# A log-sum-exp over rows: which row comes in two parts, and where its parts arrive

## The chip, the cores and the metric

The kernel runs on one core of a Trainium2 chip. The metric is the device time of one execution in microseconds (us), the median of several runs. The core has a matrix engine (PE), a vector engine (DVE), a scalar engine for exponentials and logarithms (ACT), a general engine (POOL) and a queue engine (SP) that issues the transfers (DMA) between the chip's memory and the on-chip buffer SBUF. SBUF has 128 partitions; a small second buffer, PSUM, takes PE's results and some of ACT's.

## The reference

The input is 32 x 512 rows of 1024 numbers in fp32, 64 MiB. The output is one number for each of the 16384 rows, the logarithm of the sum of the exponentials:

```python
max_x = np.max(x, axis=-1, keepdims=True)
return (max_x.squeeze(-1) + np.log(np.sum(np.exp(x - max_x), axis=-1))).astype(np.float32)
```

The kernel computes log(sum(exp(x))) without taking the maximum off, and checks beside it that the sums lie in a range where this is exact enough. Where the check fails, a second path behind a branch computes all rows again with the maximum. With this input it isn't taken.

## The kernel before

**Tiling.** Each of the 128 partitions holds 128 rows, called columns here (NC = 128), so 512 KB. Before the change the rows lie in memory as two pieces: the first 128 x 112 rows, of which each partition takes 112 in a row (W = 112; neighbouring partitions start 448 KB apart), and the last 128 x 16, of which each takes 16 (B = 16; 64 KB apart). Lines 78 to 86 make the two views of the input and of the output.

**Loads.** LOADS (lines 23 to 27) lists 18 loads with a size in columns and a string of operations. The sizes shrink towards the end, from 16 columns to 0.46875. A load may end within a row; the rest of the row then comes with the next load. All loads are issued by SP in this order (line 139), into a ring of 48 columns in SBUF. A load into a part of the ring first waits for the engine that used it last (`users`, lines 135 to 137). All loads go through one queue and their data come in the order of issue.

**Operations.** For each load ACT waits until it has landed and takes the exponential in place, one instruction for each operation of the string (line 228). The last operation of a load takes all that has landed, its partial row too. Then the rows are summed:

- `R7`: DVE sums 7 rows with one reduction (line 239).
- `F6`: POOL adds the second halves of 6 rows to the first (line 233), and DVE sums the halves later (`reduce_folded`, line 171).
- `T3`: for each of 3 rows DVE adds both halves and accumulates the sum in one instruction (line 249); PE adds the sums of the last rows into `count` for the check.
- `Y`, `Z`: the last row (column 127) comes in two loads. ACT takes the exponential of each part into PSUM and accumulates its sum, `first_sum` or `last_sum` (line 202). DVE copies `first_sum` to `sumexp` (line 212).

**Logarithms and stores.** Once column LATE = 119 is reached, ACT takes the logarithm of the first 112 columns (line 268), DVE runs the early half of the check (lines 146, 151), and SP stores these results (line 276). After the last load ACT takes the logarithm of 15 more columns (line 279), and then of the last row, where the sum of its first part comes in as the bias (line 281):

```python
ln_last = act.did(nc.scalar.activation(
    out=res[:, LAST:NC], in_=last_sum, func=AF.Ln, bias=sumexp[:, LAST:NC]
))
```

SP stores the last 16 columns (line 285), 64 bytes a partition and 8 KB in a row in memory. DVE and PE run the rest of the check (lines 290 to 308); ACT and DVE read its result, and SP waits for both (line 365), for the early store (366) and for the last one (369).

**Order.** Each engine runs its instructions in the order of the program and waits on semaphores; `Counted` counts what an engine has done, and `wait` makes another engine wait for a count.

Of the kernel before, what the change touches and what calls it, by code (L numbers as in the profile page):

```python
# [16 lines left out]
B = 16  # L17
LATE = 119
# [3 lines left out]

LOADS = [
# [29 lines left out]
def kernel(  # L53
# [5 lines left out]
    nc = tc.nc  # L59
# [24 lines left out]
    def source(e0, size):  # L84
        assert e0 >= W * d or e0 + size <= W * d
        return x_rest[:, e0 - W * d : e0 - W * d + size] if e0 >= W * d else x_rows[:, e0 : e0 + size]

    loads = [
        (int(size * d), [(op[0], 0 if op[0] == "Y" else int(op[1:] or 1)) for op in ops.split()])
        for size, ops in LOADS  # L90
    ]
    assert sum(size for size, _ in loads) == NC * d
    assert sum(s for _, ops in loads for _, s in ops) == NC
# [9 lines left out]
    over = sbuf("over", d)  # L103
# [5 lines left out]
    last_exp = nc.alloc_psum_tensor("last_exp", [P, d], fp32).ap()  # L109
# [24 lines left out]
    def load(i, here, done_before, size):  # L134
        for a, b, who, at in users:
            if a < here + size and b > here:
                sp.wait(who, at)
        users[:] = [u for u in users if not (u[0] < here + size and u[1] > here)]
        return nc.sync.dma_start(
            out=ring[:, here : here + size], in_=source(done_before, size)  # L140
        ).then_inc(landed[i], 16)

    def check_early():
        dve.wait(act, summed_by_act)
        dve.wait(dve, dve.n)
        dve.did(nc.vector.tensor_scalar(  # L146
            out=clamped[:, 0:LATE], in0=sumexp[:, 0:LATE],
            scalar1=LOW, scalar2=HIGH, op0=ALU.max, op1=ALU.min,
        ))
        dve.wait(dve, dve.n)  # L150
        dve.did(nc.vector.scalar_tensor_tensor(  # L151
            out=clamped[:, 0:LATE], in0=clamped[:, 0:LATE], scalar=0.0, in1=sumexp[:, 0:LATE],
            op0=ALU.bypass, op1=ALU.not_equal, accum_out=bad[:, 0:1],
        ))
        pe.wait(dve, dve.n)
        pe.did(nc.tensor.matmul(count, lhsT=bad[:, 0:1], rhs=far, start=True, stop=False))  # L156

# [6 lines left out]
    def reduce_folded():  # L164

        nonlocal early_sum
        while folded:
            c0, s0, p0, n0 = folded.pop(0)
            halves = ring[:, p0 : p0 + s0 * d].rearrange("p (c d) -> p c d", d=d)[:, :, 0:H]
            dve.wait(pool, n0)  # L170
            at = dve.did(nc.vector.reduce_sum(  # L171
                out=sumexp[:, c0 : c0 + s0], in_=halves, axis=AX.X
            ))
            users.append((p0, p0 + s0 * d, dve, at))
            if c0 < W:
                early_sum = at

    c = 0
    p = 0
    here = 0  # L180
    early_sum = 0
    done_before = 0
    summed_by_act = 0
    ln_early = None
    first_load = None
    for i, (size, ops) in enumerate(loads):
# [5 lines left out]
        dma = load(i, here, done_before, size)  # L192
        first_load = first_load or dma.ins
        end = here + size
        done_before += size
        act.wait(landed[i], 16)
        for k, (how, s) in enumerate(ops):
            rows = ring[:, p : p + s * d].rearrange("p (c d) -> p c d", d=d)
            if how in "YZ":

                assert c == LAST and (how == "Z" or here == p)
                at = act.did(nc.scalar.activation(  # L202
                    out=last_exp[:, here - p : end - p], in_=ring[:, here:end], func=AF.Exp,
                    accum_out=first_sum if how == "Y" else last_sum,
                ))
                if how == "Z":
                    last_piece = ring[:, here:end]
                here = end
                if how == "Y":
                    nc.vector.addr_align(128, offset=0, max_nops=0)  # L210
                    dve.wait(act, at)
                    first_piece = dve.did(nc.vector.tensor_copy(out=sumexp[:, LAST:NC], in_=first_sum))  # L212
                summed_by_act = at
            elif how == "A":
                assert here == p
                v = ring[:, p : p + d]
                at = act.did(nc.scalar.activation(
                    out=v, in_=v, func=AF.Exp, accum_out=sumexp[:, c : c + 1]
                ))
                here += d  # L220
                users.append((p, p + d, act, at))
                summed_by_act = at
                who = (act, at)
            else:
# [3 lines left out]
                at = act.did(nc.scalar.activation(out=v, in_=v, func=AF.Exp))  # L228
                here = upto
# [7 lines left out]
            elif how == "R":  # L237
                dve.wait(act, at)
                who = (dve, dve.did(nc.vector.reduce_sum(  # L239
                    out=sumexp[:, c : c + s], in_=rows, axis=AX.X  # L240
                )))
                users.append((p, p + s * d, *who))
            elif how == "T":
                if c >= W:
                    reduce_folded()
                dve.wait(act, at)
                for r in range(s):
                    lo = rows[:, r, 0:H]
                    who = (dve, dve.did(nc.vector.scalar_tensor_tensor(  # L249
                        out=lo, in0=lo, scalar=1.0, in1=rows[:, r, H:d],  # L250
                        op0=ALU.mult, op1=ALU.add, accum_out=sumexp[:, c + r : c + r + 1],
                    )))
                    users.append((p + r * d, p + (r + 1) * d, *who))
                    if c + r >= LATE:
                        add_up(c + r, who, start=False, stop=False)
            if how == "A" and c >= LATE:
                add_up(c, who, start=False, stop=False)
            if how in "RT":
                if c < W:
                    early_sum = dve.n  # L260
                reduce_folded()
            c += s
            p += s * d
            if c == LATE:

                act.wait(dve, early_sum)
                act.wait(act, early_act)
                ln_early = act.did(nc.scalar.activation(  # L268
                    out=res[:, 0:W], in_=sumexp[:, 0:W], func=AF.Ln
                ))  # L270
                check_early()
            if c <= W:
                early_act = summed_by_act
        assert here == end
    sp.wait(act, ln_early)
    nc.sync.dma_start(out=out_rows, in_=res[:, 0:W]).then_inc(sp.sem, 16)

    act.wait(dve, dve.n)
    act.did(nc.scalar.activation(out=res[:, W:LAST], in_=sumexp[:, W:LAST], func=AF.Ln))  # L279
    act.wait(act, summed_by_act)  # L280
    ln_last = act.did(nc.scalar.activation(  # L281
        out=res[:, LAST:NC], in_=last_sum, func=AF.Ln, bias=sumexp[:, LAST:NC]
    ))
    sp.wait(act, ln_last)
    nc.sync.dma_start(out=out_rest, in_=res[:, W:NC]).then_inc(stored, 16)
# [8 lines left out]
    add_up(LAST, (dve, first_piece), start=False, stop=False)  # L294
# [4 lines left out]
    half = last_piece.shape[1] // 2  # L299
# [19 lines left out]
    with nc.If(all_fine < 1):  # L319
# [5 lines left out]
        for c0 in range(0, NC, RING):  # L325
# [5 lines left out]
            edge = max(c0, min(W, c0 + s))  # L331
            for c1, c2 in ((c0, edge), (edge, c0 + s)):
                if c1 == c2:
                    continue
                nc.scalar.dma_start(
                    out=ring[:, (c1 - c0) * d : (c2 - c0) * d],
                    in_=source(c1 * d, (c2 - c1) * d),
                ).then_inc(again, 16)
                rows += 16
# [20 lines left out]
        nc.scalar.dma_start(out=out_rest, in_=res[:, W:NC]).then_inc(again, 16)  # L360
        nc.scalar.dma_start(out=out_rows, in_=res[:, 0:W]).then_inc(again, 16)
        nc.scalar.wait_ge(again, rows + 32)
# [60 lines left out]
```

## Time and profile before

| | us |
|---|---|
| median of 3 runs | 161.78 (161.76 to 161.81) |
| the profiled execution | 161.75 |
| its span, first to last instruction | 160.4 |
| ACT busy | 114.5 (71%) |
| DVE busy | 114.3 (71%) |
| POOL busy | 37.3 (23%) |
| PE busy | 2.2 (1%) |
| DMA, mean over the span | 419 GB/s |

The span is shorter than the device time by what lies around the instructions. In a list of groups, each line names the line of the kernel, the engine, the operation, what it writes and reads with the shapes, how often, the busy time, the mean of one in ns, and the idle time ahead of it with what ended it. In the chain of waits, the work that ended last is followed back from the end: each piece has its start, its duration and what ran. In the list of loads each line has the size and the time from the issue to the landing. In the waits of a queue, each line names who waited for whom: us in total, times, longest.

### The profile page before, as it was taken

To read this page: it belongs to the slowest core of one execution; us is meant where nothing else is said; L and a number is where in the kernel's file an instruction comes from. 1 tells how busy PE (TensorE), PEld (TensorE's weight loads), DVE (VectorE), ACT (ScalarE), POOL (GpSimd) and SP (SyncE) were. 2 spreads that over 40 slices of the span, in tenths; PEclk is the share of its full clock that TensorE was granted. 3 is DMA by queue.
4 is the path that set the end of the run, shared out by engine and by line. 5 is a ranking of instruction groups with operands and counts; after the bars stand their busy time and mean duration, and the time that the engine had idled before them with its cause. 6 is when DMAs were issued, how large, how long until landed. Compare 5 with 4: busy or idle time off the path is not lost.

```text
span 160.4 us, 219 instructions
## 1 busy us (share of the span) xinstructions
PE 2.2 (1%) x26; PEld 1.1 (1%) x26; DVE 114.3 (71%) x59; ACT 114.5 (71%) x31; POOL 37.3 (23%) x11
## 2 busy tenths in 40 slices
PE   0000000000000000000000000000000000000022
PEld 0000000000000000000000000000000000000011
DVE  0000000009999499994999859959999999999996
ACT  3000059990699708995099949991999989799996
POOL 0000000000000000000000994690004969891000
DMA  7996996996996996996999999999999999999992
GB/s 262 523 523 262 523 523 262 523 507 278 523 490 294 523 490 294 523 490 294 482 441 441 441 425 409 409 409 480 432 395 417 450 416 398 448 411 424 412 413 95
DMA packets 2881, 67.18 MB, mean 419 GB/s; under 512 B 576, under 2 KB 704, under 8 KB 1344
## 3 DMA queue, kind: packets, MB, share of 16 engines
q1 hardware_dynamic: 2880, 67.18, 97.7%
q14 instruction: 1, 0.01, 0.0%
HBM read 67.11 MB, written 0.07 MB: 419 GB/s over the span
## 4 chain that ended last, share of the span: by engine, by line
DMA 52%; ACT 28%; DVE 19%; issue 1%; PE 0%
DMA ring<-in_x_dram 52%; ACT ring L228 27%; DVE sumexp L239 15%; DVE sumexp L171 2%; DVE ring L249 1%; DVE over L301 0%; PE count L306 0%; ACT res L268 0%; DVE clamped L290 0%; DVE fine L308 0%; DVE sumexp L212 0%
## 5 line engine op out<-in xcount | busy, mean ns | idle before, releaser
L228 ACT ACTIVATE ring<-ring 128x16384 f32<-128x16384 f32 (+16 forms) x23 | 111.7, 4908 | 43.0 <-DMA ring<-in_x_dram 43.0
L239 DVE TENSOR_REDUCE sumexp<-ring 128x16 f32<-128x16384 f32 (+4 forms) x9 | 85.6, 9513 | 42.7 <-ACT ring L228 42.7
L233 POOL TENSOR_TENSOR ring<-ring 128x3072 f32<-128x3072 f32 (+3 forms) x7 | 37.1, 5313 | 107.3 <-ACT ring L228 107.3
L171 DVE TENSOR_REDUCE sumexp<-ring 128x6 f32<-128x3072 f32 (+3 forms) x7 | 18.4, 2656 | 0.0
L249 DVE SCALAR_TENSOR_TENSOR ring<-ring 128x512 f32<-128x512 f32 x15 | 9.6, 687 | 0.4 <-ACT ring L228 0.4
L125 ACT ACT_TABLE_LOAD x1 | 1.3, 1283 | 1.4 <-PEq L62 1.4
L156 PE MATMUL count<-far,bad 128*1 128x1 f32 x2 | 0.2, 164 | 153.2 <-DVE clamped L151 153.2
L160 PE MATMUL count<-sumexp,ones 128*1 128x1 f32 x18 | 1.6, 164 | 3.6 <-DVE ring L249 3.6
L249 DVE DVE_READ_ACCUMULATOR ring<-ring 128x1 f32 x15 | 1.2, 82 | 0.0
L202 ACT ACTIVATE last_exp<-ring 128x544 f32<-128x544 f32 (+1 forms) x2 | 1.2, 584 | 0.0
L126 DVE MEMSET ones<- 128x1 f32 x1 | 0.1, 59 | 1.5 <-PEq L62 1.5
L156 PEld LDWEIGHTS count<-far,bad 128*1 128x1 f32 x2 | 0.1, 80 | 153.2 <-DVE clamped L151 153.2
L160 PEld LDWEIGHTS count<-sumexp,ones 128*1 128x1 f32 x18 | 0.8, 80 | 4.5 <-DVE ring L249 4.5
L301 DVE SCALAR_TENSOR_TENSOR over<-ring 128x240 f32<-128x240 f32 x1 | 0.4, 404 | 0.0
L308 DVE TENSOR_SCALAR fine<-count 1x1 int32<-1x1 f32 x1 | 0.1, 147 | 0.3 <-PE count L306 0.3
L151 DVE SCALAR_TENSOR_TENSOR clamped<-clamped,sumexp 128x119 f32<-128x119 f32 x1 | 0.3, 283 | 0.0
L268 ACT ACTIVATE res<-sumexp 128x112 f32<-128x112 f32 x1 | 0.3, 279 | 0.0
L281 ACT ACTIVATE res<-last_sum,sumexp 128x1 f32<-128x1 f32 x1 | 0.3, 261 | 0.0
L202 ACT ACTIVATION_READ_ACCUMULATOR last_exp<-ring 128x1 f32 x2 | 0.3, 126 | 0.0
L146 DVE TENSOR_SCALAR clamped<-sumexp 128x119 f32<-128x119 f32 x1 | 0.2, 221 | 0.0
L279 ACT ACTIVATE res<-sumexp 128x15 f32<-128x15 f32 x1 | 0.2, 209 | 0.0
L290 DVE SCALAR_TENSOR_TENSOR clamped<-sumexp 128x9 f32<-128x9 f32 x1 | 0.2, 169 | 0.0
(17 smaller groups left out, 1.8 us busy)
## 6 DMA issues: line engine op xcount, KB each, us to landing
ring<-in_x_dram SPq DMA_DIRECT2D x1, 6912.0 KB, 23.9
ring<-in_x_dram SPq DMA_DIRECT2D x1, 6400.0 KB, 19.7
ring<-in_x_dram SPq DMA_DIRECT2D x1, 4608.0 KB, 15.9
ring<-in_x_dram SPq DMA_DIRECT2D x1, 3584.0 KB, 24.0
ring<-in_x_dram SPq DMA_DIRECT2D x1, 3072.0 KB, 19.1
ring<-in_x_dram SPq DMA_DIRECT2D x1, 2288.0 KB, 24.1
ring<-in_x_dram SPq DMA_DIRECT2D x1, 1664.0 KB, 20.9
ring<-in_x_dram SPq DMA_DIRECT2D x1, 1264.0 KB, 23.6
```

The costliest lines, as they stand in the source:

```text
L125: nc.scalar.preload_act_table_set("natural_log_exp_and_others")
L151: dve.did(nc.vector.scalar_tensor_tensor(out=clamped[:, 0:LATE], in0=clamped[:, 0:LATE], scalar=0.0, in1=sumexp[:, 0:LATE], op0=ALU.bypass ...
L156: pe.did(nc.tensor.matmul(count, lhsT=bad[:, 0:1], rhs=far, start=True, stop=False))
L160: return pe.did(nc.tensor.matmul(count, lhsT=ones, rhs=sumexp[:, c : c + 1], **kw))
L171: at = dve.did(nc.vector.reduce_sum(out=sumexp[:, c0 : c0 + s0], in_=halves, axis=AX.X))
L202: at = act.did(nc.scalar.activation(out=last_exp[:, here - p : end - p], in_=ring[:, here:end], func=AF.Exp, accum_out=first_sum if how == ...
L228: at = act.did(nc.scalar.activation(out=v, in_=v, func=AF.Exp))
L233: at = pool.did(nc.gpsimd.tensor_tensor(out=rows[:, :, 0:H], in0=rows[:, :, 0:H], in1=rows[:, :, H:d], op=ALU.add))
L239: who = (dve, dve.did(nc.vector.reduce_sum(out=sumexp[:, c : c + s], in_=rows, axis=AX.X)))
L249: who = (dve, dve.did(nc.vector.scalar_tensor_tensor(out=lo, in0=lo, scalar=1.0, in1=rows[:, r, H:d], op0=ALU.mult, op1=ALU.add, accum_out ...
L268: ln_early = act.did(nc.scalar.activation(out=res[:, 0:W], in_=sumexp[:, 0:W], func=AF.Ln))
L301: dve.did(nc.vector.scalar_tensor_tensor(out=over[:, 0:half], in0=last_piece[:, 0:half], scalar=CEILING, in1=last_piece[:, half : 2 * half ...
```

## The change

The rows lie in one piece now: each partition takes 128 rows in a row, and its neighbours start 512 KB apart, for input and output. The order in which columns are loaded changes, and LOADS names for each load where its columns come from: `front` (columns 0 to 96), `middle` (97 to 111 and the first 544 elements of column Z = 112), `late` (113 to 121 and the first 416 elements of Y = 122), `behind Y` (123 to 127), and then the rest of Y (608 elements) and the rest of Z (480). LATE is 120.

The row Z takes the place of the row that came last. Its first part comes with the fourth load (`P` under `middle`): ACT takes its exponential with the sum accumulated into `sumexp`, and then the logarithm of that sum into one more element behind the buffer `last_piece`. The last load goes into that buffer, not into the ring. Its exponential takes 481 elements: the 480 that were loaded and that logarithm, so that the accumulated sum is the whole row's; the last logarithm then needs no bias.

Another row, Y, comes in two parts as well: its first part with the load `T2 P`, where DVE adds the two halves of 208 elements and accumulates their sum, and its rest with the last load but one, where ACT accumulates and DVE adds that sum to the first (in place of the copy). The fourth load's rows are all summed by DVE (`R9 R6`, before `F9 R7`), and other loads are split anew. An alignment is added ahead of ACT's last logarithms, as DVE has one.

```diff
--- before
+++ after
...
-B = 16
-LATE = 119
...
+FRONT = 97
+Z = FRONT + 15
+Y = Z + 10
+LATE = 120
...
 LOADS = [
-    (16, "R16"), (16, "R16"), (16, "R16"), (16, "F9 R7"), (13.5, "F6 R7"), (12.5, "R7 F6"),
-    (9, "R5 F4"), (7, "F4 R3"), (6, "F2 F2 R2"), (4.46875, "T4"), (3.25, "T3"), (2.46875, "T3"),
-    (1.8125, "T2"), (1.3125, "T1"), (0.96875, "T1"), (0.71875, "T1"), (0.53125, "Y"), (0.46875, "Z"),
+    (16, "front", "R16"), (16, "front", "R16"), (16, "front", "R16"),
+    (15.53125, "middle", "R9 R6 P"), (15.75, "front", "R8 F7"), (12.25, "front", "R6 F7"),
+    (8.9375, "front", "R4 F4"), (6.9375, "front", "F4 R3"), (5.125, "front", "F4 R2"),
+    (4.09375, "late", "T4"), (3.125, "late", "T3"), (2.1875, "late", "T2 P"),
+    (1.84375, "behind Y", "T1"), (1.34375, "behind Y", "T2"), (1.03125, "behind Y", "T1"),
+    (0.78125, "behind Y", "T1"), (0.59375, "Y", "P"), (0.46875, "Z", "P"),
 ]
...
-    W = NC - B
-    LAST = NC - 1
-    x_rows = x_flat[0 : P * W].rearrange("(p c) d -> p (c d)", p=P)
-    x_rest = x_flat[P * W : n].rearrange("(p c) d -> p (c d)", p=P)
-    out_flat = out.rearrange("a b -> (a b)")
-    out_rows = out_flat[0 : P * W].rearrange("(p c) -> p c", p=P)
-    out_rest = out_flat[P * W : n].rearrange("(p c) -> p c", p=P)
...
+    x_rows = x_flat.rearrange("(p c) d -> p (c d)", p=P)
+    out_rows = out.rearrange("a b -> (a b)").rearrange("(p c) -> p c", p=P)
...
+    y_size, z_size = loads[-2][0], loads[-1][0]
...
+    to_come = {
+        "front": 0, "middle": FRONT * d, "late": (Z + 1) * d, "behind Y": (Y + 1) * d,
+        "Y": (Y + 1) * d - y_size, "Z": (Z + 1) * d - z_size,
+    }
+    column = {"front": 0, "middle": FRONT, "late": Z + 1, "behind Y": Y + 1}
...
-    over = sbuf("over", d)
+    over = sbuf("over", H)
+    last_piece = sbuf("last_piece", z_size + 1)
...
-    last_exp = nc.alloc_psum_tensor("last_exp", [P, d], fp32).ap()
+    first_exp = nc.alloc_psum_tensor("first_exp", [P, d], fp32).ap()
+    last_exp = nc.alloc_psum_tensor("last_exp", [P, H], fp32).ap()
...
-    def load(i, here, done_before, size):
+    def load(i, here, e0, size):
+        if here is None:
+            return nc.sync.dma_start(
+                out=last_piece[:, 0:size], in_=x_rows[:, e0 : e0 + size]
+            ).then_inc(landed[i], 16)
...
         return nc.sync.dma_start(
-            out=ring[:, here : here + size], in_=source(done_before, size)
+            out=ring[:, here : here + size], in_=x_rows[:, e0 : e0 + size]
         ).then_inc(landed[i], 16)
...
+        if where == "Z":
+            load(i, None, e0, size)
+            act.wait(landed[i], 16)
+            summed_by_act = act.did(nc.scalar.activation(
+                out=last_exp[:, 0 : size + 1], in_=last_piece, func=AF.Exp, accum_out=last_sum
+            ))
+            break
...
+        if where == "Y":
+            assert here == p
+            at = act.did(nc.scalar.activation(
+                out=first_exp[:, 0:size], in_=ring[:, here:end], func=AF.Exp, accum_out=first_sum
+            ))
+            p = here = end
+            nc.vector.addr_align(128, offset=0, max_nops=0)
+            dve.wait(act, at)
+            first_piece = dve.did(nc.vector.tensor_tensor(
+                out=sumexp[:, Y : Y + 1], in0=first_sum, in1=sumexp[:, Y : Y + 1], op=ALU.add
+            ))
+            continue
...
+            if how == "P" and where == "middle":
+                part = d - z_size
+                assert here == p and p + part == end
+                v = ring[:, p:end]
+                summed_by_act = act.did(nc.scalar.activation(
+                    out=v, in_=v, func=AF.Exp, accum_out=sumexp[:, Z : Z + 1]
+                ))
+                users.append((p, end, act, summed_by_act))
...
+            if how == "P":
+                half = (d - y_size) // 2
+                assert here == end and p + 2 * half == end
+                lo = ring[:, p : p + half]
+                settled = dve.did(nc.vector.scalar_tensor_tensor(
+                    out=lo, in0=lo, scalar=1.0, in1=ring[:, p + half : end],
+                    op0=ALU.mult, op1=ALU.add, accum_out=sumexp[:, Y : Y + 1],
+                ))
+                users.append((p, end, dve, settled))
...
+            c = column[where]
+            column[where] += s
...
-            if how in "YZ":
...
-                at = act.did(nc.scalar.activation(
-                    out=last_exp[:, here - p : end - p], in_=ring[:, here:end], func=AF.Exp,
-                    accum_out=first_sum if how == "Y" else last_sum,
-                ))
...
-                if how == "Y":
-                    nc.vector.addr_align(128, offset=0, max_nops=0)
-                    dve.wait(act, at)
-                    first_piece = dve.did(nc.vector.tensor_copy(out=sumexp[:, LAST:NC], in_=first_sum))
-                summed_by_act = at
...
-                upto = end if k + 1 == len(ops) and c + s < LAST else p + s * d
-                v = ring[:, here:upto]
-                at = act.did(nc.scalar.activation(out=v, in_=v, func=AF.Exp))
-                here = upto
...
+            upto = end if k + 1 == len(ops) or ops[k + 1 :] == [("P", 1)] and how == "T" else p + s * d
+            v = ring[:, here:upto]
+            if k and log_at:
+                act.wait(act, log_at)
+            at = act.did(nc.scalar.activation(out=v, in_=v, func=AF.Exp))
+            here = upto
...
-                who = (dve, dve.did(nc.vector.reduce_sum(
-                    out=sumexp[:, c : c + s], in_=rows, axis=AX.X
-                )))
...
+                at = dve.did(nc.vector.reduce_sum(out=sumexp[:, c : c + s], in_=rows, axis=AX.X))
...
+                early_sum = at
+                reduce_folded()
...
-                if c >= W:
-                    reduce_folded()
+                reduce_folded()
                 dve.wait(act, at)
                 for r in range(s):
+                    if r:
+                        dve.wait(dve, settled)
...
-            if c == LATE:
+            if c + s == LATE:
 
                 act.wait(dve, early_sum)
-                act.wait(act, early_act)
                 ln_early = act.did(nc.scalar.activation(
-                    out=res[:, 0:W], in_=sumexp[:, 0:W], func=AF.Ln
+                    out=res[:, 0:Z], in_=sumexp[:, 0:Z], func=AF.Ln
                 ))
-                check_early()
-            if c <= W:
-                early_act = summed_by_act
+                settled = check_early()
...
+        if where == "middle":
+            act.wait(act, summed_by_act)
+            log_at = act.did(nc.scalar.activation(
+                out=last_piece[:, z_size : z_size + 1], in_=sumexp[:, Z : Z + 1], func=AF.Ln
+            ))
...
-    nc.sync.dma_start(out=out_rows, in_=res[:, 0:W]).then_inc(sp.sem, 16)
+    nc.sync.dma_start(out=out_rows[:, 0:Z], in_=res[:, 0:Z]).then_inc(sp.sem, 16)
+    nc.scalar.addr_align(128, offset=0, max_nops=0)
     act.wait(dve, dve.n)
-    act.did(nc.scalar.activation(out=res[:, W:LAST], in_=sumexp[:, W:LAST], func=AF.Ln))
+    act.did(nc.scalar.activation(out=res[:, Z + 1 : NC], in_=sumexp[:, Z + 1 : NC], func=AF.Ln))
     act.wait(act, summed_by_act)
-    ln_last = act.did(nc.scalar.activation(
-        out=res[:, LAST:NC], in_=last_sum, func=AF.Ln, bias=sumexp[:, LAST:NC]
-    ))
+    ln_last = act.did(nc.scalar.activation(out=res[:, Z : Z + 1], in_=last_sum, func=AF.Ln))
     sp.wait(act, ln_last)
-    nc.sync.dma_start(out=out_rest, in_=res[:, W:NC]).then_inc(stored, 16)
+    nc.sync.dma_start(out=out_rows[:, Z:NC], in_=res[:, Z:NC]).then_inc(stored, 16)
...
-    add_up(LAST, (dve, first_piece), start=False, stop=False)
+    add_up(Y, (dve, first_piece), start=False, stop=False)
...
```

Also changed, and not shown: the second path behind the branch reads and writes the rows in one piece, and the operation `A`, which no load used, is gone.

More of the change, by code (lines that the diff above doesn't have):

```diff
@@ L181 @@
     early_sum = 0
-    done_before = 0
     summed_by_act = 0
     ln_early = None
+    log_at = 0
+    settled = 0
     first_load = None
-    for i, (size, ops) in enumerate(loads):
+    for i, (size, where, ops) in enumerate(loads):
+        e0 = to_come[where]
+        to_come[where] += size
+        if where == "Z":
[5 more added lines that the diff above has]
+            break
         if here + size > RING * d:
@@ L191 @@
             reduce_folded()
[L192 removed]
+        dma = load(i, here, e0, size)
         first_load = first_load or dma.ins
         end = here + size
[L195 removed]
         act.wait(landed[i], 16)
[L197 to L229 removed]
@@ L253 @@
-                    users.append((p + r * d, p + (r + 1) * d, *who))
+                    ))
+                    users.append((p + r * d, p + (r + 1) * d, dve, at))
                     if c + r >= LATE:
[L255 to L261, printed above, removed]
@@ L262 @@
[L262 removed]
+                        add_up(c + r, (dve, at), start=False, stop=False)
             p += s * d
[L264 removed]
+            if c + s == LATE:
                 act.wait(dve, early_sum)
[L267 removed]
                 ln_early = act.did(nc.scalar.activation(
[L269 removed]
+                    out=res[:, 0:Z], in_=sumexp[:, 0:Z], func=AF.Ln
                 ))
[L271 removed]
@@ L298 @@
     pe.did(nc.tensor.matmul(count, lhsT=less, rhs=steep, start=False, stop=False))
-    half = last_piece.shape[1] // 2
+    half = z_size // 2
     dve.wait(landed[-1], 16)
@@ L330 @@
                 nc.scalar.wait_ge(ready, steps)
[L331 to L339, printed above, removed]
+            nc.scalar.dma_start(
+                out=ring[:, 0 : s * d], in_=x_rows[:, c0 * d : (c0 + s) * d]
+            ).then_inc(again, 16)
+            rows += 16
             nc.vector.wait_ge(again, rows)
@@ L359 @@
         nc.scalar.wait_ge(ready, steps + 2)
-        nc.scalar.dma_start(out=out_rest, in_=res[:, W:NC]).then_inc(again, 16)
-        nc.scalar.dma_start(out=out_rows, in_=res[:, 0:W]).then_inc(again, 16)
-        nc.scalar.wait_ge(again, rows + 32)
+        nc.scalar.dma_start(out=out_rows, in_=res).then_inc(again, 16)
+        nc.scalar.wait_ge(again, rows + 16)
     nc.scalar.sem_inc(done, 1)
```

32 lines of the change are left out of this document (17 added, 15 removed).

## The prediction

> **What bounds the kernel now.** I read the page's chain first, then the chain in order of time, the sizes and landings of the loads, the timeline of the last two microseconds, and last the waits of SP's queue.
>
> ```profile
> DMA 52%; ACT 28%; DVE 19%; issue 1%; PE 0%
> ```
> ```profile
> 119.11 19.09 DMA ring<-in_x_dram
> 138.20 0.02 issue
> 138.22 12.34 ACT ring L228 x5
> 150.56 0.18 ACT res L268
> 150.75 6.06 ACT ring L228 x4
> ```
>
> Half of the chain is loads; from 138.22 on it is ACT alone, with no gap. That does not make ACT the only bound there. The rows of the last loads (queue, operation, KB, us from issue to landing), with the issue of the last one, show when they land:
>
> ```profile
> ring<-in_x_dram SPq DMA_DIRECT2D x1, 272.0 KB, 20.8
> ring<-in_x_dram SPq DMA_DIRECT2D x1, 240.0 KB, 20.9
> ...
> out_dram<-res SPq DMA_DIRECT2D x1, 8.0 KB, 1.4
> ```
> ```profile
> 137.02 2.22 SPq L139 DMA_DIRECT2D ring<-in_x_dram  x1
> ```
>
> The last piece (240 KB) lands at 137.02 + 20.9 = 157.9; its exponential starts at 158.01. The same sum for the nine loads before it gives 138.2, 143.6, 147.5, 150.6, 152.9, 154.5, 155.8, 156.7 and 157.4, and the exponentials start at 138.22, 143.65, 147.59, 150.66, 152.89, 154.55, 155.78, 156.71 and 157.41. Every load of the tail lands just as ACT comes free: the stream of loads and ACT are both the bound. The big loads show the stream's rate: ACT waits for them at 22.00, 41.33, 60.68 and 80.02, so 19.34 us for 16 columns of rows, 1.209 us a column, and 128 columns are 154.8 us of the span.
>
> The end, start and duration in us:
>
> ```profile
> 157.41 0.61 ACT L202 ACTIVATE last_exp<-ring 128x544 f32<-128x544 f32 x1
> ...
> 158.01 0.56 ACT L202 ACTIVATE last_exp<-ring 128x480 f32<-128x480 f32 x1
> 158.16 0.15 DVE L212 COPY sumexp<-first_sum 128x1 f32<-128x1 f32 x1
> 158.56 0.21 ACT L279 ACTIVATE res<-sumexp 128x15 f32<-128x15 f32 x1
> 158.67 0.26 ACT L281 ACTIVATE res<-last_sum,sumexp 128x1 f32<-128x1 f32 x1
> 158.95 0.34 SPq L285 DMA_DIRECT2D out_dram<-res  x1
> 159.13 0.15 DVE L308 TENSOR_SCALAR fine<-count 1x1 int32<-1x1 f32 x1 [0.28 <-PE count L306]
> ```
> ```profile
> SPq L367 <- ACTq L364: 0.7, 1, 0.7
> SPq L369 <- SPq L369: 0.3, 1, 0.3
> ```
>
> After the last landing come the exponential, two logarithms, and a store of 1.4 us: 158.95 + 1.4 = 160.35, the span's end. The check (L290 to L308) runs beside it, and SP still waits 0.3 us for the store once the check is through: that is the check's cover.
>
> **The change part by part.** *ACT's price list.* Exponentials of 16384 and 2048 elements take 13.857 and 1.899 us, so 0.834 ns an element and 0.19 us fixed; the next one starts some 0.09 us before the end of one, so each adds 0.834 ns an element + 0.10. An early logarithm adds 0.19 (150.47 to 150.66), a read of the accumulator 0.05 (157.41 to 158.01 for 544 elements is 0.60; by the formula 0.55).
>
> *The row's first part in the fourth load* (544 elements). It adds to ACT one exponential (0.64), its accumulator (0.13) and a logarithm (0.2), about 1 us, at about 92.5 to 93.5: the fourth load lands at 79.4, R9 and R6 take 7.9 + 5.2, and the fifth, which now completes 79.28 columns, lands near 98.5. ACT would be idle for those 5 us anyway, as it was 5.5 us before each big load. Without that cover it would cost 1 us. Cost 0.
>
> *DVE, POOL and the ring.* Seven more rows go through DVE's full reduction (1.07 us each) and seven fewer through POOL's fold and the half reduction (0.54): about +3.6 us of DVE. The prices (shape, count, then busy us and mean ns):
>
> ```profile
> L239 DVE TENSOR_REDUCE sumexp<-ring 128x7 f32<-128x7168 f32 x3 | 22.9, 7617 | 3.9 <-ACT ring L228 3.9
> ...
> L171 DVE TENSOR_REDUCE sumexp<-ring 128x6 f32<-128x3072 f32 x2 | 6.7, 3344 | 0.0
> ```
>
> Seven whole rows 7.62, and 5, 3 and 2 in the rows beside them 5.49, 3.34 and 2.27: 1.068 us a row and 0.14. Six half rows 3.34, and 9, 4 and 2 of them 4.94, 2.27 and 1.21: 0.539 a row and 0.13. Each starts some 0.08 before the end of the one ahead. Chaining from 91.7, the end of the third R16, R9 R6 R8 end at 116.5; R6 waits for its exponential until 118.1; then R6, F7, R4, F7, F4, R3, F4, R2, F4 end at 148.8 (before: 147.74). POOL, 2.12 ns an element, ends each fold just ahead of its turn (131.9 for 132.7, 136.7 for 136.7, 146.3 for 146.6). From there DVE has no gap: 7 rows at 0.613, the early check 0.58, two rows, the half row (0.30, from L301's 240 elements at 0.33), five rows: 158.3. Then the add for Y, 0.15 like the copy it replaces: 158.45, 0.14 later than the copy ended; the check behind it moves by as much, inside its 0.3. The logarithm of 15 columns can't start before ACT is done with the last exponential, at 158.57. So DVE has 0.1 us to spare, the least of any part; late by more, it takes the logarithms and the store with it.
>
> *SP's queue* (load i is entry i of LOADS, from 0). Load 7 now waits for R8 (116.5, was 106.9) and load 9 for the fold of the fifth load (128.4, was 119.5). When they are issued, loads until 124.2 and 138.8 are still on the way: 7 us of cover. Load 17 has its own buffer and no wait. Cost 0.
>
> *The tail on ACT.* Interpolating the landings above at the new sums of columns: 138.8, 143.8, 147.6, 150.3, 152.6, 154.3, 155.6, 156.6, 157.4, 157.9. ACT's instructions in this stage go from 12 to 11, and load 8 is 5.125 columns. Start by start, the later of landing + 0.03 and ACT free: 138.87, 143.84, 147.62, then 150.58 (held by the early logarithm), 152.62, 154.31, 155.61, 156.60, Y at 157.38, and 64 elements more in it than before put the last at 158.03 (before 158.01). +0.02.
>
> *Y's add and the bias.* The last logarithm loses its per-partition bias. No row shows it so. From both sides: it stays 0.26, or it costs the fixed 0.19 less the 0.03 by which the row of 480 elements into PSUM is under the formula: 0.16. I take 0.18, between an input in SBUF and one in PSUM: −0.08. Waiting for Y's sum moves from the bias to the logarithm before it, which waited for that copy already.
>
> *The stores.* The last one now writes 64 bytes at a pitch of 512 instead of 8 KB in one run. No row shows such a store; the nearest is the one it replaces, 64 bytes from each partition too. By the busy share of the DMA engines its data move at 159.75 to 160.00, 0.8 us after the issue, and it lands 0.35 later. Only those 0.35 us can depend on where the bytes go: −0.35 if they vanished, +0.35 if they doubled; I take 0, the amount of data and the number of pieces being the same. The early store changes its addresses too, but it is queued behind the loads and lands at 150.78 + 7.4 = 158.2, 0.7 before the last store is issued; without that cover it would take the difference with it. ACT's alignment adds a branch ahead of the logarithm, under the last exponential; DVE had one in its tail and no gap shows there. 0, at most the 0.15 of a short instruction.
>
> *128 rows in one piece.* Each partition's source now lies 512 KB from the next; before, it was 448 KB for 112 columns and 64 KB for 16. Bounds: the big loads at 448 KB give 1.209 us a column; the first load at 64 KB took 5.43 us for 4.469 columns, 1.215, and part of that is its smaller size. So 0 to 0.5%, 0 to 0.8 us over 154.8. I take 0: 448 is the nearest row by far. The Trainium skill speaks against it: "DMA: Bandwidth & Descriptors", section "Latency and other measured facts", lists copies between tensors in memory at a row pitch of 512 KiB with 207 GB/s a direction, and 214 as the full rate. By that, 154.8 us of loads would take 5.2 more; no trace here has that pitch.
>
> **Sum.** +0.02 − 0.08 = −0.06 on the profiled execution, 161.75 with a span of 160.4; the median of the runs is 0.03 above that execution. **161.7 us**, no change that can be told: 0.2% of 161.78 is 0.32 us, about what a measurement of this kernel can tell.
>
> **The rivals.**
> *The pitch slows the stream* (slower, 25%). For it: the loads run through the whole span, any loss sits straight on the end, and the tail's loads are met just in time. Against: 448 KB and 64 KB show one rate. Each 1% costs 1.55 us; it decides from 0.2%. At the row bound of 0.5%, 162.5; at 2%, 164.8. By the figures of the Trainium skill's page, 3.4%, it would be 166.9.
> *DVE late* (10%). If the stage from 91.7 takes 1% more (0.65 us), it eats the 0.1 and pushes the logarithms: 161.7 + 0.55 = 162.2, with the check past its 0.3 too. For it: the margin is 0.1 after 66 us chained from rows. Against: every row used is of the same engine and form.
> *The scattered store costs* (7%): its 0.35 doubles, with the branch's 0.15 not hidden: 162.2.
> *The end gains more* (6%): the store's 0.35 falls by three quarters, 161.7 − 0.26 = 161.4, the edge of faster. For it: separate lines of memory for each piece; against: no row shows pieces hindering each other.
> *The parts don't bite:* the stream bounds the end and the bias was free: 161.8. It falls within the forecast.
>
> **How the numbers follow.** Forecast with that last one, 52%, its own range 161.5 to 162.0. The range 161.4 to 162.9 takes in DVE, the branch and the pitch up to 0.8 us (about 10 of its 25); left out are the pitch beyond (15%) and a little at the low end. Slower by over 0.2%: pitch 25, DVE 9, branch and store 5 = 39%. Faster: 6%. Same: 55%.
>
> **What would show it.** The waits of ACT for the second and third load: 19.3 us apart if the pitch is free, 19.7 at 2%. The last exponential starts at 158.0 with its landing 0.05 ahead; the logarithm of 15 columns follows it without a wait for DVE; the last logarithm takes 0.18. A wait of ACT for the Y add, or for loads 1 to 5 at a wider spacing, would make the prediction wrong.

## The result, and the profile after

| | before | after |
|---|---|---|
| median, us | 161.75 (161.60 to 161.81, 8 runs) | 162.17 (161.87 to 162.58, 8 runs) |
| ratio | | 1.003, interval 1.0017 to 1.0044 |
| the profiled execution, its span | 161.75, 160.4 | 162.54, 161.2 |

The change made the kernel slower by 0.3%, some 0.4 us. The forecast was 161.7 and no change that can be told; the time lies in the forecast's range, but the interval of the ratio lies above 1. The profiled execution is one of the slow ends of the spread (162.54 against the median of 162.17), so its 0.8 us of span are more than the usual loss.

The chain of waits of the changed kernel now names DVE where ACT stood; that is no sign of a slower DVE, whose rows fill the tail almost without a gap in both kernels and which, as the end further down shows, was done before ACT:

```profile
DMA 39%; DVE 30%; ACT 22%; another core or an unknown queue 3%; POOL 3%; issue 0%; PE 0%
```

What went wrong is seen at the other end of the execution. ACT's first waits for loads, from the timeline of ACT (start, duration, instruction, and in brackets the idle time ahead of it and what ended it), before:

```profile
22.00 13.86 ACT L228 ACTIVATE ring<-ring 128x16384 f32<-128x16384 f32 x1 [19.27 <-DMA ring<-in_x_dram]
41.33 13.86 ACT L228 ACTIVATE ring<-ring 128x16384 f32<-128x16384 f32 x1 [5.46 <-DMA ring<-in_x_dram]
```

and after:

```profile
22.41 13.86 ACT L262 ACTIVATE ring<-ring 128x16384 f32<-128x16384 f32 x1 [19.68 <-DMA ring<-in_x_dram]
41.73 13.86 ACT L262 ACTIVATE ring<-ring 128x16384 f32<-128x16384 f32 x1 [5.46 <-DMA ring<-in_x_dram]
61.07 13.86 ACT L262 ACTIVATE ring<-ring 128x16384 f32<-128x16384 f32 x1 [5.49 <-DMA ring<-in_x_dram]
79.84 13.10 ACT L262 ACTIVATE ring<-ring 128x9216 f32<-128x9216 f32 x2 [4.92 <-DMA ring<-in_x_dram]
99.47 13.73 ACT L262 ACTIVATE ring<-ring 128x8192 f32<-128x8192 f32 x2 [5.65 <-DMA ring<-in_x_dram]
```

The first three loads are the same in both kernels, 16 columns each. They come 19.32 and 19.34 us apart in the changed kernel, as before, so no rate is lost between them; but the first one is 0.41 late, and those that follow are late with it. The fifth is 0.98 late against the same schedule with a good start (98.49, in e11 below): in this execution 0.6 more came in mid-stream. The lateness reaches the end:

```profile
158.85 0.57 ACT L207 ACTIVATE last_exp<-last_piece 128x481 f32<-128x481 f32 x1
...
159.12 0.15 DVE L228 TENSOR_TENSOR sumexp<-first_sum,sumexp 128x1 f32<-128x1 f32 x1
...
159.39 0.21 ACT L310 ACTIVATE res<-sumexp 128x15 f32<-128x15 f32 x1
...
159.50 0.17 ACT L312 ACTIVATE res<-last_sum 128x1 f32<-128x1 f32 x1
...
159.70 0.34 SPq L314 DMA_DIRECT2D out_dram<-res  x1
```
```profile
last_piece<-in_x_dram SPq DMA_DIRECT2D x1, 240.0 KB, 25.6
out_dram<-res SPq DMA_DIRECT2D x1, 8.0 KB, 1.5
```
```profile
133.15 7.35 SPq L147 DMA_DIRECT2D last_piece<-in_x_dram  x1
```

The last load lands at 133.15 + 25.6 = 158.75 instead of 157.9, and its exponential starts 0.84 later than before. Behind it things went as forecast: Y's add on DVE ends at 159.27, before the logarithm of 15 columns could start, and the last logarithm takes 0.17 instead of 0.26.

### The profile page after: what moved, and what is told of

The parts are those of the page before. It is cut to its first block, busy times and chain, and to the rows that moved or that the text cites. A ratio compares the mean times of both kernels' runs of the same rounds, so it can differ in the third digit from the quotient of the medians.

```text
span 161.2 us, 216 instructions
## 1 busy us (share of the span) xinstructions
PE 2.0 (1%) x24; PEld 1.0 (1%) x24; DVE 117.2 (73%) x58; ACT 115.0 (71%) x33; POOL 29.4 (18%) x9
## 4 chain that ended last, share of the span: by engine, by line
DMA 39%; DVE 30%; ACT 22%; another core or an unknown queue 3%; POOL 3%; issue 0%; PE 0%
DMA ring<-in_x_dram 39%; ACT ring L262 22%; DVE sumexp L273 20%; DVE ring L284 5%; DVE sumexp L187 4%; POOL ring L267 3%; DVE over L330 0%; DVE ring L247 0%; DVE clamped L166 0%; DVE clamped L161 0%; PE count L335 0%; DVE clamped L319 0%; DVE fine L337 0%; DVE sumexp L228 0%
## 5 line engine op out<-in xcount | busy, mean ns | idle before, releaser
L262 ACT ACTIVATE ring<-ring 128x16384 f32<-128x16384 f32 (+18 forms) x22 | 111.4, 5101 | 43.2 <-DMA ring<-in_x_dram 43.0
L273 DVE TENSOR_REDUCE sumexp<-ring 128x16 f32<-128x16384 f32 (+6 forms) x10 | 93.0, 9321 | 40.9 <-ACT ring L262 40.9
L267 POOL TENSOR_TENSOR ring<-ring 128x2048 f32<-128x2048 f32 (+1 forms) x5 | 29.2, 5842 | 117.6 <-ACT ring L262 117.6
L187 DVE TENSOR_REDUCE sumexp<-ring 128x4 f32<-128x2048 f32 (+1 forms) x5 | 14.6, 2918 | 0.2 <-POOL ring L267 0.2
L284 DVE SCALAR_TENSOR_TENSOR ring<-ring 128x512 f32<-128x512 f32 x14 | 8.8, 684 | 0.0
L222 ACT ACTIVATE first_exp<-ring 128x608 f32<-128x608 f32 x1 | 0.7, 663 | 0.0
L237 ACT ACTIVATE ring<-ring 128x544 f32<-128x544 f32 x1 | 0.6, 641 | 0.0
L207 ACT ACTIVATE last_exp<-last_piece 128x481 f32<-128x481 f32 x1 | 0.6, 566 | 0.0
## 6 DMA issues: line engine op xcount, KB each, us to landing
ring<-in_x_dram SPq DMA_DIRECT2D x1, 2624.0 KB, 22.4
```

The lines of the kernel that those rows point to most:

```text
L187: at = dve.did(nc.vector.reduce_sum(out=sumexp[:, c0 : c0 + s0], in_=halves, axis=AX.X))
L207: summed_by_act = act.did(nc.scalar.activation(out=last_exp[:, 0 : size + 1], in_=last_piece, func=AF.Exp, accum_out=last_sum))
L222: at = act.did(nc.scalar.activation(out=first_exp[:, 0:size], in_=ring[:, here:end], func=AF.Exp, accum_out=first_sum))
L237: summed_by_act = act.did(nc.scalar.activation(out=v, in_=v, func=AF.Exp, accum_out=sumexp[:, Z : Z + 1]))
L267: at = pool.did(nc.gpsimd.tensor_tensor(out=rows[:, :, 0:H], in0=rows[:, :, 0:H], in1=rows[:, :, H:d], op=ALU.add))
L273: at = dve.did(nc.vector.reduce_sum(out=sumexp[:, c : c + s], in_=rows, axis=AX.X))
```

## The experiments

Theory P said that the 512 KB between neighbouring partitions lets DMA engines fall behind, theory O that the new order, sizes and buffer of the loads do. All times are medians; the kernel before ran beside each on the same chip. ACT "meets" a load when it starts on it after a wait; the times of these meetings come from one profiled execution of each kernel.

**Pieces put back, and one piece alone.** e1 is the changed kernel with two pieces, e2 the kernel before with one; e3 is the kernel before with two pieces of 64 columns; e4 repeats the changed kernel. Core of e1, of e2 and of e3:

```diff
-    x_rows = x_flat.rearrange("(p c) d -> p (c d)", p=P)
+    S = FRONT
+    x_rows = x_flat[0 : P * S].rearrange("(p c) d -> p (c d)", p=P)
+    x_rest = x_flat[P * S : n].rearrange("(p c) d -> p (c d)", p=P)
```
```diff
-    x_rows = x_flat[0 : P * W].rearrange("(p c) d -> p (c d)", p=P)
-    x_rest = x_flat[P * W : n].rearrange("(p c) d -> p (c d)", p=P)
...
+    x_rows = x_flat.rearrange("(p c) d -> p (c d)", p=P)
```
```diff
-    x_rows = x_flat[0 : P * W].rearrange("(p c) d -> p (c d)", p=P)
-    x_rest = x_flat[P * W : n].rearrange("(p c) d -> p (c d)", p=P)
+    S = 64
+    x_rows = x_flat[0 : P * S].rearrange("(p c) d -> p (c d)", p=P)
+    x_rest = x_flat[P * S : n].rearrange("(p c) d -> p (c d)", p=P)
```

> The changed kernel with its rows in two pieces again, split at column 97 (neighbouring partitions 388 KB and 124 KB apart), and one early store more; loads, sizes, order and tail unchanged. Theory P (the 512 KB pitch lets some DMA engines fall behind at moments, and the tail waits for the last one): about 161.65 us, that is 0.05 to 0.15 under before, runs within 0.3 us of each other, and the last load lands near 157.9 as before. Theory O (the new sizes, order or buffer of the loads are to blame): 162.1 to 162.2 as the changed kernel, the last landing near 158.7.

> The kernel before with its rows in one piece (512 KB pitch for the input and for both stores), nothing else changed. Theory P: 162.1 to 162.4 us, runs spread over 0.5 us or more, the last landing 0.3 to 0.9 later than 157.9, and ACT idle in the tail. Theory O: 161.75, as before. If only the scattered last store cost time: 161.8, with the last landing unmoved and that store 0.05 to 0.1 longer.

> The kernel before with its rows in two pieces of 64 columns (256 KB pitch in both, so another power of two), one early store more. Theory P in the form that any large power of two hurts: 161.9 to 162.1 us. In the form that 512 KB hurts and smaller pitches don't: 161.75. Theory O: 161.75.

> The changed kernel once more, on the same chip as the other three: 162.0 to 162.3 us with runs spread over 0.5 us. Theory P: the profile of this other execution shows landings late by another amount and from another moment on than the first one (there: 0.4 from the first load, 0.95 from the fifth), since it is chance which engines fall behind. Theory O: the same lateness at the same loads.

| | us | before beside it | ratio, interval |
|---|---|---|---|
| e1, changed, 388 and 124 KB | 161.72 | 161.63 | 1.000, 0.9991 to 1.0009 |
| e2, before, 512 KB | 162.32 | 161.63 | 1.0037, 1.0023 to 1.005 |
| e3, before, 256 KB twice | 161.76 | 161.63 | 1.0007, 0.9998 to 1.0016 |
| e4, changed, 512 KB | 162.32 | 161.63 | 1.0032, 1.0022 to 1.0042 |

Theory O falls: the layout alone brings the loss into the old schedule (e2) and its return takes it out of the new one (e1). A power of two as such does no harm at 256 KB. In e4 the first load was met at 22.33 and the fifth at 99.16: late again, by other amounts than in the first profile.

The views time a load as a whole, but the traces also record when each of its 16 parts lands. In all 16 profiled executions on record the first part of the first load lands 21.2 to 21.5 us after the start. The last part follows 0.40 to 0.73 later where the rows of that load lie at most 480 KB apart, and 0.76 to 1.00 later at 496 and 512 KB. From the first load to the last the gap changes little: from 0.53 to 0.51 in the kernel before, from 0.96 to 0.92 in e5 and from 0.95 to 0.79 in e6 below. In the first profile of the changed kernel it grew on the way, from 1.00 to 1.47 at the fifth load, and was 1.30 at the last. So some parts fall behind the others and stay behind, as theory P has it of the DMA engines; the trace doesn't say which engine moved which part.

**Which loads.** e5 reads the kernel before in pieces of 124 and 4 columns (496 KB), a distance that is no power of two. e6 reads only the first load at 512 KB, e7 all but the first:

```diff
+    S = 124
+    x_high = x_flat[0 : P * S].rearrange("(p c) d -> p (c d)", p=P)
+    x_low = x_flat[P * S : n].rearrange("(p c) d -> p (c d)", p=P)
```
```diff
+    x_one = x_flat.rearrange("(p c) d -> p (c d)", p=P)
     def source(e0, size):
+        if e0 < 16 * d:
+            return x_one[:, e0 : e0 + size]
```
```diff
+    x_one = x_flat.rearrange("(p c) d -> p (c d)", p=P)
     def source(e0, size):
+        return x_rows[:, e0 : e0 + size] if e0 < 16 * d else x_one[:, e0 : e0 + size]
```

> The kernel before with its input read as two pieces of 124 and 4 columns (neighbouring partitions 496 KB and 16 KB apart); the stores are as before, so results land in other rows' places. If it is the power of two that makes engines fall behind: 161.65 us, the first load landing near 22.0 and the last near 157.9. If it is the width of the pitch, so that 448 KB is just under a limit: 162.1 or more, with the first load near 22.3.

> The kernel before, only the first load (16 columns) read at the 512 KB pitch, so that some rows are read in place of others; everything else as before. In the runs with one piece so far the first load landed at 22.2 to 22.4 instead of 22.0. If that part is the start's own (all engines begin at once, on rows 512 KB apart): 161.95 us, the first load 0.3 later and all others later by the same, for what an engine has lost is not regained. If the losses come from loads in full flight: 161.65.

> The complement: the first load at 448 KB, all 17 others at the 512 KB pitch (some rows read in place of others). If the loss is the start's alone: 161.65 us. If loads in full flight lose too: 161.9 to 162.1, the first load at 22.0, the last 0.2 to 0.5 later than 157.9. The two should add up to the 0.69 us that the kernel before lost with one piece throughout.

All three beside 161.64: e5 162.20 (1.0034, 1.0024 to 1.0044), e6 162.11 (1.0029, 1.0019 to 1.0039), e7 161.65 (1.0001, 0.9992 to 1.001). It is not the power of two. The loss is the first load's: 17 loads at 512 KB cost nothing behind a first one at 448 KB. The same view of ACT's waits: the sixth load of the kernel before, then e6 and e7:

```profile
111.50 18.89 ACT L228 ACTIVATE ring<-ring 128x6656 f32<-128x6656 f32 x4 [3.32 <-DMA ring<-in_x_dram]
```
```profile
22.33 13.86 ACT L232 ACTIVATE ring<-ring 128x16384 f32<-128x16384 f32 x1 [19.60 <-DMA ring<-in_x_dram]
41.65 13.86 ACT L232 ACTIVATE ring<-ring 128x16384 f32<-128x16384 f32 x1 [5.46 <-DMA ring<-in_x_dram]
...
111.82 18.91 ACT L232 ACTIVATE ring<-ring 128x6656 f32<-128x6656 f32 x4 [3.31 <-DMA ring<-in_x_dram]
```
```profile
21.88 13.86 ACT L229 ACTIVATE ring<-ring 128x16384 f32<-128x16384 f32 x1 [19.15 <-DMA ring<-in_x_dram]
41.19 13.86 ACT L229 ACTIVATE ring<-ring 128x16384 f32<-128x16384 f32 x1 [5.45 <-DMA ring<-in_x_dram]
...
111.38 18.88 ACT L229 ACTIVATE ring<-ring 128x6656 f32<-128x6656 f32 x4 [3.33 <-DMA ring<-in_x_dram]
```

In e6 the lateness stays that of the first load: against the kernel before, 22.33 − 22.00 and 111.82 − 111.50 are 0.33 and 0.32, and the last exponential starts at 158.38, 0.37 late. In e7 no load is late. The parts were expected to add up and don't: 0.47 and 0.01 against 0.69 for one piece throughout. The difference is the later lateness: in e2 the first load is met 0.26 late, the sixth 0.44 late, and the last exponential starts 0.67 late (158.68).

```profile
22.26 13.86 ACT L225 ACTIVATE ring<-ring 128x16384 f32<-128x16384 f32 x1 [19.53 <-DMA ring<-in_x_dram]
...
111.94 18.94 ACT L225 ACTIVATE ring<-ring 128x6656 f32<-128x6656 f32 x4 [3.43 <-DMA ring<-in_x_dram]
```

In the profiled executions this later lateness appears only where both the first load and the others are at 512 KB. Why it needs both is not shown.

**What about the first load, and is it all?** In e10 the two pieces change places in memory, so that the first load reaches into the last 8 MiB at 448 KB; e11 is the changed kernel with only its first load at 448 KB; e12 and e13 are the kernel before with only the first load at 480 and 64 KB. Core of e10, e11, e12 and e13 (in the last two `source` sends the first load there, as in e6):

```diff
-    x_rows = x_flat[0 : P * W].rearrange("(p c) d -> p (c d)", p=P)
-    x_rest = x_flat[P * W : n].rearrange("(p c) d -> p (c d)", p=P)
+    x_rows = x_flat[P * B : n].rearrange("(p c) d -> p (c d)", p=P)
+    x_rest = x_flat[0 : P * B].rearrange("(p c) d -> p (c d)", p=P)
```
```diff
+    x_first = x_flat[0 : P * Z].rearrange("(p c) d -> p (c d)", p=P)
...
-            out=ring[:, here : here + size], in_=x_rows[:, e0 : e0 + size]
+            out=ring[:, here : here + size], in_=(x_rows if i else x_first)[:, e0 : e0 + size]
```
```diff
+    x_one = x_flat[0 : P * 120].rearrange("(p c) d -> p (c d)", p=P)
```
```diff
+    x_head = x_flat[0 : P * B].rearrange("(p c) d -> p (c d)", p=P)
```

> The kernel before with its two pieces exchanged: the 112 columns are the last 56 MiB of the input, the 16 columns the first 8 MiB; distances between rows stay 448 and 64 KB. If the first load is slow because it reaches into the last 8 MiB: 162.1 us, first load at 22.3. If it is slow because of the distance between rows: 161.65, first load at 22.0.

> The changed kernel, only its first load read with rows 448 KB apart (some rows read in place of others). If the start is the changed kernel's whole loss: 161.7 us, first load at 21.9, all engines' landings within 0.6 us to the end. If its other loads at 512 KB lose as well, as its profile showed from the fifth load on: 161.9 to 162.1, the first load at 21.9 and the last 0.2 to 0.5 later than 157.9.

> The kernel before, only the first load read with rows 480 KB apart (some rows read in place of others). A limit between 448 and 480: 162.1 us as with 512. A limit between 480 and 496, or the last 2 MiB of the input: 161.65. A gradual growth with the distance: near 161.9.

> The kernel before, only the first load read with rows 64 KB apart, one run of 8 MiB (some rows read in place of others). If the start grows slower with distance over the whole range: 161.4 us or less, first load before 21.8, under both kernels. If there is only a limit near 480 KB: 161.65.

Beside 161.69: e10 161.69 (0.9998, 0.9989 to 1.0007), e11 161.58 (0.9992, 0.9983 to 1.0001), e12 161.80 (1.0009, 1.0 to 1.0018), e13 161.75 (0.9999, 0.999 to 1.0008). The distance between the rows decides, not the place in memory; how far a whole load is spread over memory grows with that distance, and these runs don't separate the two. At 496 KB the loss is there in full (e5, which has it on all loads but the last few); at 480 the interval just touches 1, and that profile's first load was met on time, at 22.00, so what little there may be isn't settled; nothing is gained below 448. And one line of the changed kernel, which load the stream starts with, takes its whole loss away. Its waits and its end in e11:

```profile
22.05 13.86 ACT L264 ACTIVATE ring<-ring 128x16384 f32<-128x16384 f32 x1 [19.32 <-DMA ring<-in_x_dram]
...
98.49 13.74 ACT L264 ACTIVATE ring<-ring 128x8192 f32<-128x8192 f32 x2 [5.03 <-DMA ring<-in_x_dram]
```
```profile
157.89 0.57 ACT L209 ACTIVATE last_exp<-last_piece 128x481 f32<-128x481 f32 x1
...
158.55 0.17 ACT L314 ACTIVATE res<-last_sum 128x1 f32<-128x1 f32 x1
158.74 0.34 SPq L316 DMA_DIRECT2D out_dram<-res  x1
159.15 0.15 DVE L339 TENSOR_SCALAR fine<-count 1x1 int32<-1x1 f32 x1 [0.28 <-PE count L337]
```

**What the change's own parts are worth.** e8 is the changed kernel with pieces of 112 and 16 columns (the fourth load in two transfers, the stores as before), e9 the same without the alignment on ACT, e14 the changed kernel with pieces of 48 and 80 columns:

```diff
+    S = Z
...
+        if e0 < S * d < e0 + size:
+            whole = S * d - e0
+            nc.sync.dma_start(
+                out=ring[:, here : here + whole], in_=source(e0, whole)
+            ).then_inc(landed[i], 16)
+            return nc.sync.dma_start(
+                out=ring[:, here + whole : here + size], in_=source(S * d, size - whole)
+            ).then_inc(landed[i], 16)
```
```diff
-    nc.scalar.addr_align(128, offset=0, max_nops=0)
```
```diff
-    S = FRONT
+    S = 48
```

(e8 against the changed kernel, with its two views as in e1; e9 against e8; e14 against e1.)

> The changed kernel with pieces of 112 and 16 columns as the kernel before has them: the fourth load comes as two transfers, 15 columns from the one piece and the 544 elements of the split row from the other; the stores are those of the kernel before (64 bytes a partition, 8 KB in one run). The first try with two pieces issued its last store 0.17 us before the kernel before did, but that store took 1.6 us instead of 1.4; there each partition's 64 bytes began at a multiple of 124, not of 64. If that is what the store paid for: store 1.4 us and 161.45 to 161.55 us, under both kernels. If the second fetch of instructions near the end (ACT's alignment) holds the store up: store still 1.5 to 1.6, 161.65. If the split transfer costs the stream: last landing 0.1 later, 161.65.

> The same without the alignment ahead of ACT's last logarithms. If its fetch of instructions delays the store: the fetch is gone or elsewhere, the store takes 1.4 us and the time is 0.1 less than with it. If it is free: the same time within 0.05. If the alignment guards against a stall of ACT at the end: slower by 0.1 or more, with a gap ahead of a logarithm or of the read of the check's result.

> The changed kernel with its rows in two pieces of 48 and 80 columns (neighbouring partitions 192 and 320 KB apart), so that the first load starts with near rows, no load is cut, and the last store begins at multiples of 64 bytes; one early store more. If the start was all that the change lost: 161.5 to 161.65 us, 0 to 0.15 under the kernel before, the last landing near 157.85 and the last store issued near 158.75. If the early split row costs something that the near start only hid in e11: 161.7 or more.

e8 161.69 (1.0004, 0.9993 to 1.0014) and e9 161.68 (1.000, 0.9991 to 1.0009) beside 161.68; e14 161.57 (0.9997, 0.9988 to 1.0006) beside 161.67. No version can be told from the kernel before. One execution of e8 took 162.50 and one of e14 162.12, the other ten of each at most 161.86 and 161.63; neither of the two was profiled, so what made them long is open. The last stores explain part of why nothing is gained (start and duration of the issue; KB and us to landing), e8 and then e9:

```profile
158.59 0.34 SPq L330 DMA_DIRECT2D out_dram<-res  x1
```
```profile
out_dram<-res SPq DMA_DIRECT2D x1, 8.0 KB, 1.7
```
```profile
158.64 0.34 SPq L329 DMA_DIRECT2D out_dram<-res  x1
```
```profile
out_dram<-res SPq DMA_DIRECT2D x1, 8.0 KB, 1.4
```

Both issue it 0.3 to 0.4 before the 158.95 of the kernel before. With the alignment it takes 0.3 longer in e8, and 1.6 in e1 and e14; without it 1.4, and yet the time is the same: e9's span ended at 160.1 but its execution took 161.66, 1.56 more, where the others take 1.3 to 1.4 more than their span. So the alignment is neither a cost nor a gain here. That it makes the store slow is not settled, as e11 has it and a store of 1.4. The addresses are not the reason: e1's begin at multiples of 124 bytes and e8's at multiples of 64, and e2's scattered store took 1.4.

## Why the prediction was right or wrong

**The step that failed** is "128 rows in one piece", taken at 0. The bounds of 0 to 0.8 us held the loss (0.4 to 0.69 by run), but the value and its shape were wrong; since the bounds were drawn for a loss of rate, it is luck that they held. I read the price of the distance from rows of loads in full flight, 448 and 64 KB, and priced a rate. No loss of rate shows: the first three big loads stay 19.3 us apart. What the runs showed is a price of the start: the first load, which no row priced apart, lands 0.2 to 0.4 late at 496 and 512 KB, and the stream that runs without a gap to the end never regains it. With 512 KB throughout, a price in mid-stream came on top, 0.6 at the fifth load in one execution. The sign that was named for a price, the spacing of the second and third load, stayed at 19.3 us while the change cost time, for it can't see a late start; a wider spacing came only at the fifth load, 19.63 us behind the fourth against 18.99 in e11. The first load's own landing was in the profile, and I used it only as the origin from which spacings were counted.

**The rival** named for it came true in its sign and near the low end of its price, with another mechanism. The Trainium skill's page "DMA: Bandwidth & Descriptors", section "Latency and other measured facts", has 512 KiB at 207 GB/s against 214. The measurement decides: no loss of rate shows in e7, and far from the 5.2 us that the figures give, the whole layout cost 0.69. Its advice against such a pitch would have been right here; that a few KB of padding are enough, as it says, was not tried, and 496 KB, no power of two, cost 0.56.

**The tail on ACT**: forecast +0.02 for the last exponential from unchanged landings. In e11, where the landings are near unchanged, it started at 157.89, 0.12 before the kernel before, inside what the landings themselves vary.

**Y's add and the bias**: forecast 0.18 for the last logarithm, measured 0.17.

**DVE**: forecast to start the last rows at 148.8 and to end with Y's add at 158.3 to 158.45; in e11 148.73, and the add started at 158.18. The rival "DVE late" did not happen.

**The early logarithm and the first part of the row**: nothing, as forecast; e11 holds it all and loses nothing.

**The stores**: 1.5 in the changed kernel, 1.4 in e2 with the same addresses, against 1.4 forecast.

**The sum** of −0.06 without the layout stands within what can be told: e11 −0.11 and e14 −0.10 by their medians, both intervals with 1 in them. A step I left out caps it: in e11 SP has no wait for the last store left, while it waits for the check for longer (before: 0.7, and then 0.3 for the store):

```profile
SPq L392 <- ACTq L389: 0.9, 1, 0.9
```

The check's last instruction came at 159.15, in the kernel before at 159.13. In e11 the check and not the store sets the end; in e1 and e14, whose store took 1.6, SP still waits 0.3 for the store.

## What to carry to other kernels

A spacing between equal loads shows the rate, not the start: where the stream of loads runs without a gap from the first instruction to the last, compare also when the first load lands, for a late start is paid in full at the end. When a layout changes, test it on the first load alone and on all but the first; two runs told here what the whole kernel could not. A saving behind the last load is worth only as much as the next path to the end leaves.

## What had not been expected of the hardware

The first load of 16 columns landed 0.2 to 0.4 us later with neighbouring partitions 496 or 512 KB apart than in the kernel before (met at 22.2 to 22.4, and at 480 KB and less at 21.8 to 22.1), because the last of its 16 parts came later while the first came as early as ever. Later loads at 512 KB came at the same 19.3 us. With 512 KB throughout, further losses came in mid-stream, 0.6 at the fifth load in one execution of the changed kernel and at other loads in others, and its times spread over 0.7 us where the kernel before spread over 0.2; behind a start at 448 KB the same loads at 512 KB showed none (e7, e11). What in the memory does this was not tried.
